# Conditioned decoder trunk on one Trainium2 core: c loaded as columns and broadcast through TensorE, and the first FFN weights in two transfers per k-tile

## The chip, the core and the metric

The kernel runs on one core of one Trainium2 chip. A core has a matrix engine (TensorE, PE in the profile; its weight loads are PEld), a vector engine (VectorE, DVE), a scalar engine (ScalarE, ACT), a general engine (GpSimd, POOL) and a sync engine (SyncE, SP) that here issues nearly all transfers between HBM and on-chip memory. Each engine works through its own list of instructions in order; engines wait for one another, and for transfers, through semaphores. The metric is the device time of one execution in microseconds; 1000.66 us is the median of three executions before the change (999.98 to 1000.76).

## The reference, cut to what matters

Two layers act on x, 256 positions by 1024 channels, all in float32. Each layer is FFN, token mixer, FFN; every sub-layer normalises x, modulates it with a shift and a scale computed from one conditioning vector c, and adds its result through a gate computed from c.

```python
c_act = silu(c)                                  # c: (1, 1024)
mods = c_act @ ada_w[layer] + ada_b[layer]       # nine vectors of 1024 a layer
sh1, sc1, g1, ... = split(mods, 9)
h = rms_norm(x, norm_g) * (1 + sc1) + sh1
x = x + 0.5 * g1 * swiglu(h, w_gate, w_up, w_down)
h = ...                                          # sh2, sc2
x = x + g2 * attention(h)                        # layer 0: MoBA, layer 1: MLA
h = ...                                          # sh3, sc3
x = x + 0.5 * g3 * swiglu(h, ...)
```

The change touches the beginning: silu(c), the shift and the scale of the very first norm, and the first 768 of 2816 columns of the first FFN's gate and up matrices.

## The kernel before

Every float32 product is done with operands split into a rounded high part (`hi`, type float32r) and a remainder (`lo`); ACT makes the high part by a copy and DVE the remainder by a subtraction (`split`, L624 to L629). Weights stream from HBM in 1 MB tiles through three buffers (`rawp`, tag `raw`; `wload`, L727). The matrices for shift, scale and gate stream in 512 KB tiles (`adaw`); a shift or scale column is a DVE product of such a tile with c_b, which holds silu(c) on all 128 partitions, summed along the row (`column`, L635).

The order on each engine isn't the order of the code. `Order` (L244) lists all instructions with their dependences, gives each a modelled cost (`duration`, L199), places them one after the other on the engine that is free first, and fixes the resulting order per engine. `ranked(j)` gives instructions of the beginning a rank that overrides their due time. One item of that model is the cost of a change of ACT's function table, `TABLE` (1280 ns), added whenever the planned function needs the other table (L454 to L456).

The beginning is `first` (L1490). For the first six blocks of 128 FFN columns, gate and up, it works k-tile by k-tile (eight k-tiles of 128 channels), so that work can start as soon as the first k-tile has arrived. In a k-tile stand:

- loads on SP: two `adaw` tiles (shift, scale; 512 KB each, L1523) and the k-tile's weights (`load_w`, L1510), 128 x 1536 elements in three transfers of 256 KB. They lie in pieces of six borrowed buffers, in the places `3 * (k % 6) + j`, so k-tiles 6 and 7 reuse the places of 0 and 1;
- on DVE: two products with c_b (`column`, L1578; the instruction's line is L638), a small one for the scale (L643), then three remainders `wlo` of the weights (L1591) and the remainder of h (L773);
- on ACT: three high parts `whi` (L1590), the modulation `z` of the transposed x (L1581), the high part of h (L772), and for every second k-tile the scaling `y` of x (L1568);
- on PE: 36 products of 256 columns (L1599 to L1601) into six PSUM banks that zero products (L1540) have opened, and the transposes of x (L1564 for the first two k-tiles, by a product with a diagonal matrix `diag` that holds 1/rms; L1569 for the others).

c reaches c_b as follows: a 1 x 1024 row is loaded on ACT's queue (L1515), silu is applied to the row on one partition (L1528), PE multiplies a column of ones with the row, 512 columns at a time (L1532), and ACT copies the two halves from PSUM to c_b (L1533). A second copy of c, in columns (`cact`, 128 x 8, part of the tile `cols`), has its own silu (L1534) and is used by the gates. The norm of x needs a sum of squares for each half t of the positions: t=0 on DVE (L1550), t=1 on ACT (L1547) with a small DVE instruction behind it (L1548); POOL turns them into 1/rms (L794) and ACT into `diag` (L1554).

In the ranks, k-tile k's weights have 2k+3 and its `adaw` tiles 2k+2, but the loads and splits of k-tiles 6 and 7 have rank 2 * KD + 2 = 18, behind the `adaw` tiles of k-tile 7 (rank 16). The 1 MB tiles of the rest of the FFN come after them and need a `raw` buffer that `first` has given back.

## Time and profile before

| | |
|---|---|
| median of three executions | 1000.66 us |
| the profiled execution's own time | 1000.38 us |
| its span, first to last instruction | 998.6 us |
| PE busy | 984.3 us, 99% |
| DVE, ACT, POOL busy | 848.7, 630.1, 82.8 us |
| read from HBM | 255.34 MB, 260 GB/s over the span |

The profile is one execution, taken by the hardware profiler. In the views that follow, a timeline row reads: start in us, length in us, engine (a q behind it means that only the engine's sequencer works: it issues a transfer), line, operation, output tile, input tiles, shape, count of instructions merged, and in brackets how long the engine had been idle and what ended that. A row of the waits reads: who, for whom, us in total, times, longest. A row of the windows gives the busy time of each engine in a stretch of time, then the share of the clock, the busy share of the DMA engines and GB/s.

### The profile page before, as it was taken

The numbers are of one execution on the slowest core, as the hardware profiler recorded it, in microseconds if no ns is written. First come the engines' busy times: TensorE is split into PE (matmuls) and PEld (weight loads), VectorE is DVE, ScalarE is ACT, GpSimd is POOL, SyncE is SP. The second block draws the span as 40 slices with busy tenths as digits, with TensorE's granted clock in tenths as the row PEclk, the third lists the DMA queues.
The fourth block names the chain that finished last, engine by engine and source line by source line (L and its number), as shares of the span: only waits on it lengthen the run. The fifth ranks groups of instructions, "written<-read, shape, count | busy, mean of one in ns | idle before, by whom it ended". The sixth has DMA issues, their size and how long they took to land.

```text
span 998.6 us, 15267 instructions
## 1 busy us (share of the span) xinstructions
PE 984.3 (99%) x5558; PEld 837.0 (84%) x5558; DVE 848.7 (85%) x1442; ACT 630.1 (63%) x1171; POOL 82.8 (8%) x124
## 2 busy tenths in 40 slices
PE   8999999999999999999999999999999999999998
PEld 6988888888888788888888888888888878888886
DVE  7999999799989899999799999944998789677542
ACT  6698564378755876665367665633879686667421
POOL 1012100022230000000000000000143010000000
PEclk9999999999999999999999999999999999999999
DMA  9979989799786679988988989752343467544630
GB/s 366 402 263 298 334 315 347 303 334 350 269 299 238 237 277 331 333 302 317 363 326 315 331 320 326 235 215 98 106 153 127 170 243 273 201 169 170 230 127 21
DMA packets 54237, 260.53 MB, mean 261 GB/s; under 512 B 6289, under 2 KB 6801, under 8 KB 35986
## 3 DMA queue, kind: packets, MB, share of 16 engines
q1 hardware_dynamic: 52704, 255.93, 70.5%
q0 software_dynamic: 1024, 3.17, 1.1%
q8 instruction: 43, 0.70, 0.3%
q10 hardware_dynamic: 434, 0.46, 0.2%
q14 instruction: 32, 0.26, 0.1%
HBM read 255.34 MB, written 4.19 MB: 260 GB/s over the span
## 4 chain that ended last, share of the span: by engine, by line
PE 79%; issue 9%; DVE 6%; DMA 4%; POOL 1%; ACT 1%; SPq 0%; ACTq 0%; DVEq 0%; POOLq 0%
PE mm L957 23%; PE mm L757 12%; PE mm L759 12%; PE mm L758 12%; PE mm L965 12%; DMA adaw<-in_ada_dram 2%; PE at L1013 2%; DVE lo L628 2%; DMA raw<-in_first_dram 1%; PE at L1069 1%; PE at L1049 1%; PE tr L1168 1%; PE tr L807 1%; DMA raw<-in_w_dram 1%; DVE z L823 0%
## 5 line engine op out<-in xcount | busy, mean ns | idle before, releaser
L628 DVE TENSOR_TENSOR lo<-raw,hi 128x1024 fp32r<-128x1024 f32 (+3 forms) x312 | 368.9, 1199 | 71.8 <-ACT hi L627 63.2
L627 ACT ACTIVATE hi<-raw 128x1024 fp32r<-128x1024 f32 (+3 forms) x312 | 318.7, 1038 | 154.2 <-PE mm L759 124.2
L957 PE MATMUL mm<-h,hi 128*128 128x512 f32 x1120 | 288.3, 393 | 0.0
L957 PEld LDWEIGHTS mm<-h,hi 128*128 128x128 f32 x1120 | 199.9, 189 | 34.8
L965 PEld LDWEIGHTS mm<-h,lo 128*128 128x128 f32 x1120 | 155.3, 190 | 12.8 <-DVE lo L628 0.8
L965 PE MATMUL mm<-h,lo 128*128 128x256 f32 x1120 | 162.0, 282 | 0.6 <-DVE lo L628 0.6
L638 DVE CUSTOM_DVE_ANT_0 adaw<-adaw,c_b,cols 128x1024 f32<-128x1024 f32 x112 | 142.0, 1285 | 2.5 <-DMA adaw<-in_ada_dram 1.5
L757 PE MATMUL mm<-hi,gh 128*128 128x512 f32 x352 | 137.3, 390 | 0.0
L759 PE MATMUL mm<-hi,gl 128*128 128x512 f32 x352 | 137.1, 389 | 0.0
L758 PE MATMUL mm<-lo,gh 128*128 128x512 f32 x352 | 137.0, 389 | 0.0
L757 PE MATMUL mm<-hi,h 128*128 128x512 f32 (+1 forms) x240 | 94.7, 400 | 0.8 <-ACT h L772 0.8
L759 PE MATMUL mm<-hi,h 128*128 128x512 f32 (+1 forms) x240 | 92.6, 391 | 1.6 <-DVE h L773 1.6
L758 PE MATMUL mm<-lo,h 128*128 128x512 f32 (+1 forms) x240 | 93.8, 394 | 0.0
L759 PEld LDWEIGHTS mm<-hi,gl 128*128 128x128 f32 x352 | 66.1, 188 | 13.8
L758 PEld LDWEIGHTS mm<-lo,gh 128*128 128x128 f32 x352 | 66.1, 188 | 13.5
L757 PEld LDWEIGHTS mm<-hi,gh 128*128 128x128 f32 x352 | 66.1, 188 | 13.3
L676 DVE SCALAR_TENSOR_TENSOR acc<-adaw,cols,acc 128x1024 f32<-128x1024 f32 x48 | 61.8, 1288 | 0.3
L759 PEld LDWEIGHTS mm<-hi,h 128*128 128x128 f32 x240 | 45.1, 188 | 10.5 <-DVE h L773 2.1
L757 PEld LDWEIGHTS mm<-hi,h 128*128 128x128 f32 x240 | 45.0, 188 | 9.5 <-ACT h L772 1.4
L758 PEld LDWEIGHTS mm<-lo,h 128*128 128x128 f32 x240 | 45.1, 188 | 8.1 <-issue 0.2
L895 ACT ACTIVATE u<-mm 128x256 f32<-128x256 f32 x70 | 26.3, 375 | 32.7 <-PE mm L965 31.7
L772 ACT ACTIVATE gh<-g 128x256 fp32r<-128x256 f32 x76 | 31.4, 413 | 24.4 <-DVE g L899 24.1
(233 smaller groups left out, 1235.1 us busy)
## 6 DMA issues: line engine op xcount, KB each, us to landing
raw<-in_w_dram SPq DMA_DIRECT2D x142, 1024.0 KB, 5.2
adaw<-in_ada_dram SPq DMA_DIRECT2D x160, 512.0 KB, 5.8
raw<-in_first_dram SPq DMA_DIRECT2D x24, 256.0 KB, 7.3
raw<-in_w_dram SPq DMA_DIRECT2D x12, 512.0 KB, 3.5
raw<-in_w_dram SPq DMA_DIRECT2D x6, 576.0 KB, 3.8
bias_d<-bt SPq DMA_DIRECT2D x12, 256.0 KB, 5.5
bg<-bias_d POOLq DMA_DIRECT2D x4, 768.0 KB, 6.4
raw<-in_w_dram SPq DMA_DIRECT2D x2, 768.0 KB, 4.1
```

Source lines behind the costliest of these rows:

```text
L627: nc.scalar.activation(hi, src, AF.Copy)
L628: nc.vector.tensor_tensor(lo, src, hi.bitcast(F32), op=ALU.subtract)
L638: nc.vector.tensor_tensor_reduce(wt, wt, c_b, 1.0, cols[:, i, c:c + 1], op0=ALU.mult, op1=ALU.add, accum_out=m_cols[:, i, c:c + 1])
L676: nc.vector.scalar_tensor_tensor(acc, ada_tile(j, k), cact[:, k:k + 1], acc, op0=ALU.mult, op1=ALU.add)
L757: nc.tensor.matmul(ps, lh, rh, start=start, stop=False)
L758: nc.tensor.matmul(ps, lh, rl, start=False, stop=False)
L759: nc.tensor.matmul(ps, ll, rh, start=False, stop=stop)
L772: nc.scalar.activation(hi, ps, AF.Copy)
L895: nc.scalar.activation(x, ps[:, S:], AF.Copy)
L957: nc.tensor.matmul(ps[i], w[0], hs[2], start=k == 0, stop=False)
L965: nc.tensor.matmul(ps[i][:, S:], w, hk_, start=False, stop=k == KD - 1)
L1013: nc.tensor.matmul(ps3[:, i, :], qTs(e, t), kTs(e, nk), start=bias is not None, stop=bias is not None or i == len(es) - 1)
```

## The change

- c is laid out on the host as 128 rows of 8 values, `cact` becomes a tile of its own, loaded by a transfer of its own on ACT's queue; c is no longer part of `cols`.
- silu is applied once, to `cact`. c_b is made by eight products of 128 columns: the stationary operand is one column of `cact` repeated 128 times, the moving one the identity. The two copies to c_b stay.
- The first weights come in two transfers per k-tile, 1024 and 512 columns (k-tile 0 in three of 512), and their splits have the same pieces. Their places change: k-tiles 6 and 7 no longer lie in the places of 0 and 1 but in those of 3, 4 and 2, and only three, not four k-tiles are loaded without a wait for a norm's instruction.
- Loads and splits of k-tiles 6 and 7 have the ranks of their place: load k+3 is ranked 2k+10 = 2(k+3)+4, split 2k+3.
- In the planner, a table change costs only what ACT's idle time before it doesn't hide.

The planner makes a new order for the whole kernel from this. On PE it has 64 places of difference, on ACT 53, on DVE 139, on SP 25, none on POOL.

```diff
@@ lay_out
-    out["first"] = out["first"].reshape(KD, P, 3, -1).transpose(0, 2, 1, 3)
+    first = out["first"].reshape(KD, P, -1)
+    out["first"] = np.concatenate([first[:, :, :FIRST_A].reshape(KD, -1), first[:, :, FIRST_A:].reshape(KD, -1)], axis=1)
...
-    more = [v["c"].reshape(KD, P).T, pos.view(np.float32).reshape(NT, P).T]
+    out["c"] = v["c"].reshape(KD, P).T
+    more = [pos.view(np.float32).reshape(NT, P).T]
@@ Order.place
             if self.table[k] and self.table[k] != table:
                 table = self.table[k]
-                occ, dur = occ + TABLE, dur + TABLE
+                d = max(0.0, TABLE - (t - idle_from))
+                occ, dur = occ + d, dur + d
...
+            if e == "Activation":
+                idle_from = free[e]
@@ first
-            third = n1 // 3
+            cuts = (0, FIRST_A, n1)
...
-            place = [t[:, c:c + third] for t in raws for c in range(0, t.shape[-1], third)]
+            place = [(r[:, :FIRST_A], r[:, FIRST_A:n1]) for r in raws[:3]]
+            place += [(raws[3 + b], raws[b][:, n1:]) for b in range(3)]
+            place += [(raws[3 + b], raws[2][:, b * 512:(b + 1) * 512]) for b in range(2)]
 
             def load_w(k):
-                for j in range(3):
-                    nc.sync.dma_start(w1(k, j), a["first"][k, j])
+                for w, c, e in zip(place[k], cuts, cuts[1:]):
+                    src = a["first"][k, c * P:e * P].rearrange("(p f) -> p f", p=P)
+                    step = 512 if k == 0 else e - c
+                    for c1 in range(0, e - c, step):
+                        nc.sync.dma_start(w[:, c1:c1 + step], src[:, c1:c1 + step])
 
             with ranked(0):
-                nc.scalar.dma_start(c_b[0:1, :], a["c"])
+                nc.scalar.dma_start(cact, a["c"])
                 nc.scalar.dma_start(all_cols, a["cols"])
...
-                if k < 4:
+                if k < 3:
                     with ranked(2 * k + 3):
                         load_w(k)
             with ranked(0):
-                nc.scalar.activation(c_b[0:1, :], c_b[0:1, :], AF.Silu)
+                nc.scalar.activation(cact, cact, AF.Silu)
                 for i in range(2):
                     pt = tr_tile()
-                    half = slice(i * 512, (i + 1) * 512)
-                    nc.tensor.matmul(pt, ones[0:1, :], c_b[0:1, half], start=True, stop=True)
-                    nc.scalar.activation(c_b[:, half], pt, AF.Copy)
-                nc.scalar.activation(cact, cact, AF.Silu)
+                    for j in range(4):
+                        k = 4 * i + j
+                        nc.tensor.matmul(kslice(pt, j), cact[:, k:k + 1].to_broadcast([P, P]), ident, start=True, stop=True)
+                    nc.scalar.activation(c_b[:, i * 512:(i + 1) * 512], pt, AF.Copy)
...
-            for k in (4, 5):
+            for k in (3, 4, 5):
                 with ranked(2 * k + 3):
                     load_w(k)
...
-                with ranked(2 * k + 3 if k < KD - 2 else 2 * KD + 2):
+                with ranked(2 * k + 3):
                     hi, lo = [fp.tile([P, n1], F32R, tag=g, name=nm(g), bufs=2) for g in ("whi", "wlo")]
-                    for j in range(3):
-                        cs = slice(j * third, (j + 1) * third)
-                        nc.scalar.activation(hi[:, cs], w1(k, j), AF.Copy)
-                        nc.vector.tensor_tensor(lo[:, cs], w1(k, j), hi.bitcast(F32)[:, cs], op=ALU.subtract)
-                if k < 2:
-                    with ranked(2 * KD + 2):
-                        load_w(KD - 2 + k)
+                    for w, c, e in zip(place[k], cuts, cuts[1:]):
+                        step = 512 if k == 0 else e - c
+                        for c1 in range(c, e, step):
+                            cs, src = slice(c1, c1 + step), w[:, c1 - c:c1 - c + step]
+                            nc.scalar.activation(hi[:, cs], src, AF.Copy)
+                            nc.vector.tensor_tensor(lo[:, cs], src, hi.bitcast(F32)[:, cs], op=ALU.subtract)
+                if k in (3, 4):
+                    with ranked(2 * k + 10):
+                        load_w(k + 3)
```

Line numbers below are those of the kernel before; behind the change the same lines stand 7 to 10 further down (L1591 becomes L1601, L638 becomes L645).

What the new order does with the instructions around the change, engine by engine, as the two programs list them:

| engine | before | after |
|---|---|---|
| ACT | load c, load cols, table, silu of the row, silu of cact, square of x (t=1), two copies to c_b, diag, diag, whi x3, z, h | load c, load cols, table, silu of cact, two copies to c_b, square of x (t=1), diag, diag, whi, z, h, whi x2 |
| DVE | ..., the small instruction of t=1 (L1548), column, column, scale, wlo x2, h, wlo | the same small instruction (now L1556), column, column, scale, wlo, h, wlo x2 |
| DVE, first 1 MB tile | lo, 18 other instructions, lo | lo, 2 other instructions, lo |
| SP, end of `first` | adaw of k 6, adaw of k 7, weights of k 6 and 7, 1 MB tile, three adaw tiles, two 1 MB tiles | adaw of k 6, weights of k 6, adaw of k 7, weights of k 7, two 1 MB tiles, three adaw tiles, a 1 MB tile |

More of the change, by code (lines that the diff above doesn't have):

```diff
@@ L31 @@
 B1 = 6
+FIRST_A = 1024
 H = 16
@@ L167, in lay_out @@
     out["tab"] = np.concatenate([*[np.tile(x, (4, 1)) for x in (table[1:], table[:-1], end)], *keys], axis=1)
-    for n in ("x", "c", "positions", "kv_a_norm_g", "mla_q_a_norm_g"):
+    for n in ("x", "positions", "kv_a_norm_g", "mla_q_a_norm_g"):
         out[n] = v[n]
@@ L377, in place @@
             in_pool[r[0]] = in_pool.get(r[0], 0) + users[t]
-        flight, dma_free, dtype, table = [], 0.0, None, None
+        flight, dma_free, dtype, table, idle_from = [], 0.0, None, None, 0.0
         def grant(r):
@@ L610, in trunk @@
     pos_f = a["positions"].rearrange("o s -> (o s)")
-    all_cols = cp.tile([P, 3 * NK + KD + NT + 4 + 2 * RO], F32, name="cols")
+    all_cols = cp.tile([P, 3 * NK + NT + 4 + 2 * RO], F32, name="cols")
+    cact = cp.tile([P, KD], F32, name="cact")
     places = {}
     c0 = 3 * NK
-    for name, n in (("c", KD), ("pos", NT), ("moba_q", 1), ("moba_k", 1), ("q", 1), ("q_pe", RO), ("k", 1), ("k_pe", RO)):
+    for name, n in (("pos", NT), ("moba_q", 1), ("moba_k", 1), ("q", 1), ("q_pe", RO), ("k", 1), ("k_pe", RO)):
         places[name] = all_cols[:, c0:c0 + n]
         c0 += n
-    cols, cact = all_cols[:, :3 * NK].rearrange("p (i c) -> p i c", i=3), places["c"]
+    cols = all_cols[:, :3 * NK].rearrange("p (i c) -> p i c", i=3)
     m_cols = cp.tile([P, 2, NK], F32, name="m_cols")
```

2 lines of the change are left out of this document (removed).

## The prediction

> **What bounds the kernel now.** I read the page first: how much of the span PE is busy.
>
> ```profile
> span 998.6 us, 15267 instructions
> PE 984.3 (99%) x5558; PEld 837.0 (84%) x5558; DVE 848.7 (85%) x1442; ACT 630.1 (63%) x1171; POOL 82.8 (8%) x124
> ```
>
> PE leaves 14.3 us of the span unused, so that's all that an edit which removes no product can win. Where these lie is asked of the windows of the beginning and of PE's own waits, over the whole span and then in 700 to 830, the MLA stage, which gave the same three rows.
>
> ```profile
> core 0: us, PE busy (x) PEld busy (x) DVE busy (x) ACT busy (x) POOL busy (x), PEclk, DMA share, GB/s
> 14.00:18.00 4.00, 4.00 (x36) 4.00 (x35) 4.00 (x10) 2.73 (x5) 0.00 (x0) 1.00 1.04 403
> 38.00:42.00 4.00, 3.50 (x29) 3.29 (x28) 4.00 (x9) 1.87 (x4) 0.00 (x0) 1.00 1.06 392
> 50.00:54.00 4.00, 3.37 (x22) 2.83 (x20) 4.00 (x15) 3.30 (x8) 1.12 (x32) 1.00 0.96 386
> ```
>
> ```profile
> PE mm L759 <- DVE h L773: 1.6, 2, 1.4
> ...
> PE mm L757 <- ACT ckT L772: 0.6, 1, 0.6
> PE mm L757 <- ACT qlT L772: 0.6, 1, 0.6
> ```
>
> In `first`, PE, DVE and the DMA engines are all full at once (4.00 of 4.00 us, share 1.04, 403 GB/s): three limits within a few per cent of one another. PE idles 0.50 us in 38 to 42 and 0.63 us in 50 to 54. The largest waits of PE outside the beginning are in the MLA stage (the L757 and L759 rows, 2.8 us together). The rest of the 14.3 us lies mostly ahead of the first real product. So I read the timeline of the first 13 us, by engine.
>
> ```profile
> 0.74 0.52 ACTq L1515 DMA_DIRECT2D c_b<-in_c_dram  x1
> ...
> 1.69 1.28 ACT L1528 ACT_TABLE_LOAD   x1 [1.69 <-PEq L1641]
> 2.98 1.05 ACT L1528 ACTIVATE c_b<-c_b 1x1024 f32<-1x1024 f32 x1
> 4.09 3.78 PE L1532 MATMUL tr<-c_b,ones_r 1*128 1x512 f32 x4 [1.05 <-ACT c_b L1528]
> 4.39 1.22 DVE L1550 CUSTOM_DVE_ANT_0 raw<-x 128x1024 f32<-128x1024 f32 x1 [2.10 <-DMA x<-in_x_dram]
> 6.09 0.21 ACT L1534 ACTIVATE cols<-cols 128x8 f32<-128x8 f32 x1 [2.06 <-DMA cols<-in_cols_dram]
> 6.21 1.04 ACT L1547 ACTIVATE raw<-x 128x1024 f32<-128x1024 f32 x1
> 7.25 1.25 ACT L1533 ACTIVATE c_b<-tr 128x512 f32<-128x512 f32 x2
> 7.37 0.15 DVE L1548 TENSOR_SCALAR ssq<-ssq 128x1 f32<-128x1 f32 x1 [1.12 <-ACT raw L1547]
> 8.54 1.28 DVE L638 CUSTOM_DVE_ANT_0 adaw<-adaw,c_b,cols 128x1024 f32<-128x1024 f32 x1 [1.01 <-ACT c_b L1533]
> 8.84 2.08 PE L1564 MATMUL tr<-diag,x 128*128 128x128 f32 x8
> 9.24 1.97 ACT L1590 ACTIVATE whi<-raw 128x512 fp32r<-128x512 f32 x3 [0.16 <-DMA raw<-in_first_dram]
> 11.02 1.28 DVE L1591 TENSOR_TENSOR wlo<-raw,whi 128x512 fp32r<-128x512 f32 x2
> 11.21 0.56 ACT L1581 ACTIVATE z<-tr,m_cols 128x256 f32<-128x256 f32 x1
> 11.80 0.42 ACT L772 ACTIVATE h<-z 128x256 fp32r<-128x256 f32 x1
> ...
> 12.27 1.22 PE L1599 MATMUL mm<-h,whi 128*128 128x256 f32 x4 [0.29 <-ACT h L772]
> ```
>
> The chain: silu of the row to 4.03, products to 7.87, copies to 8.50, DVE's columns from 8.54, 2.48 us for two of them and the scale, then z, h and the first product at 12.27. From 8.54 on DVE has hardly a pause until the last remainder.
>
> ```profile
> 13.20 1.28 DVE L638 CUSTOM_DVE_ANT_0 adaw<-adaw,c_b,cols 128x1024 f32<-128x1024 f32 x1
> 15.68 1.29 DVE L1591 TENSOR_TENSOR wlo<-raw,whi 128x512 fp32r<-128x512 f32 x2
> 17.25 0.68 DVE L1591 TENSOR_TENSOR wlo<-raw,whi 128x512 fp32r<-128x512 f32 x1
> 17.86 1.28 DVE L638 CUSTOM_DVE_ANT_0 adaw<-adaw,c_b,cols 128x1024 f32<-128x1024 f32 x1
> 27.25 0.43 DVE L773 TENSOR_TENSOR h<-z,h 128x256 fp32r<-128x256 f32 x1 [0.88 <-ACT h L772]
> 44.96 2.49 DVE L1591 TENSOR_TENSOR wlo<-raw,whi 128x512 fp32r<-128x512 f32 x4
> 47.59 1.22 DVE L628 TENSOR_TENSOR lo<-raw,hi 128x1024 fp32r<-128x1024 f32 x1
> 52.67 1.22 DVE L628 TENSOR_TENSOR lo<-raw,hi 128x1024 fp32r<-128x1024 f32 x1
> ```
>
> A k-tile costs DVE 4.66 us (13.20 to 17.86); its one real pause is 0.88 us at k-tile 3; the last remainder ends at 47.45.
>
> **The change part by part.**
>
> *c to c_b.* When the 128 rows of 8 values land isn't in the trace. From below: silu can't start before the table is loaded, 2.97. From above: x's first half is asked for in the same instant and its consumer starts at 4.39. I take 3.5, a little under the middle, since c is 4 KB and x 512 KB. Silu on 128x8 costs 0.21 (the L1534 row), so PE starts at 3.75. The L1564 row is four products of this size, each two passes: eight passes in 2.08 us. Eight products are twice that less one drain, 3.6 us: nothing is won against 3.78. The first copy now finds ACT free, the second (0.62) ends at 8.05 instead of 8.50: 0.45 early (ends 7.5 and 8.95).
>
> *What is moved behind it.* In the new order ACT does both copies ahead of the square of x (L1547), and on DVE the small L1548 of that square still stands ahead of the first column. So the columns now wait for copies plus square: 8.05 + 1.13 (6.21 to 7.34) + 0.1 = 9.3, against 8.54. **0.75 us later**, although c_b is earlier. The diagonal of t=1 follows at about 10.4 and is hidden by the columns, which end at 11.8.
>
> *k-tile 0.* ACT now does z and h ahead of the second and third whi: z 11.9, h 12.45, whi to 14.05, so DVE's third wlo ends near 14.85 and k-tile 1's columns start at 14.75 instead of 13.20: **1.55 late**, half of it new. PE's first product comes at 12.95 instead of 12.27.
>
> *Two pieces instead of three.* One remainder of 1024 costs 1.22 (the L628 row) against 1.29 for two of 512: 0.07 us for each of seven k-tiles, **-0.5 us**. Two transfers instead of three save SP an issue per k-tile; that is worth nothing, for SP stands waiting for earlier transfers to land:
>
> ```profile
> SPq L1512 <- DMA adaw<-in_ada_dram: 12.9, 13, 2.4
> ```
>
> *The order of the weights.* Whi's waits for these weights, and what SP and PE do at the end of `first`:
>
> ```profile
> ACT whi L1590 <- DMA raw<-in_first_dram: 7.8, 7, 2.1
> ```
>
> ```profile
> 38.72 0.33 SPq L734 DMA_DIRECT2D raw<-in_w_dram  x1
> ...
> 46.32 1.48 SPq L734 DMA_DIRECT2D raw<-in_w_dram  x2
> ```
>
> ```profile
> 50.84 2.00 PE L957 MATMUL mm<-h,hi 128*128 128x512 f32 x8
> 52.68 0.63 PE L965 MATMUL mm<-h,lo 128*128 128x256 f32 x4
> 53.94 0.74 PE L965 MATMUL mm<-h,lo 128*128 128x256 f32 x4 [0.63 <-DVE lo L628]
> ```
>
> The bytes are the same and DMA was full, so nothing lands sooner in total. But DVE comes 1.55 us later to k-tile 1 and 1.3 later to k-tile 3, so its pause there is filled: **-0.9 us**. DVE's last remainder: 47.45 + 1.55 - 0.5 - 0.9 = 47.6, 0.15 later than before. Behind it PE had 3.4 us left (47.45 to 50.84), some 30 products at the 0.11 us that 36 records in 4.00 us give. Now k-tile 6's weights arrive before k-tile 7's columns, and PE has only k-tile 7 at the end: 36 products, of which six or so fit between h and the last remainder (0.7 us). Again 30: no gain. The cover of PE's pause at 41 (0.50) is DVE, which ends last either way.
>
> The gain lies right behind. Two 1 MB tiles go out before DVE is done with k-tile 7, instead of one (38.72) with the next held to 46.32, and DVE's second lo stands two instructions behind the first instead of eighteen. The 0.63 us wait at 53.94 goes: **-0.6 us**. If the second tile were still late, nothing would be won there; if it also helped the next blocks, up to 1.1 us.
>
> *Third load of k-tile 6 and 7 on SP.* They now wait for k-tiles 3 and 4 to be split. By the DVE times above k-tile 3's wide remainder ends near 28, about 1 us before SP would issue at the DMA's pace; nothing, as long as DVE isn't another 1 us late.
>
> *The planner's new price for tables.* The table loads stay five and in their places. The reordered instructions in the MLA stage meet the 2.8 us of waits quoted above: bounds -2.8 and, if the new order lengthens them as much, +2.8. A handful of products moved by a few places either way: I take **-0.3**.
>
> *Sum* against the profiled execution, 1000.38: DVE's end +0.15, behind it -0.6, MLA -0.3, together -0.75: 999.63. The median stands 0.28 above that execution: **999.9 us**.
>
> **The rivals.** (A) c takes turns with x and lands with its first half, 4.4. For it: cols, asked for right behind x's second half, is consumed at 6.09, x's half at 6.21. Columns then start at 10.2; 0.9 of DVE time is added: 1000.8.
>
> The Trainium skill (DMA: Bandwidth & Descriptors, section Queues, rings and completion order) says that each DMA engine takes turns between queue rows, a packet from each. By that rule c would be done with x's first half, 1000.8; the pair 6.09 and 6.21 agrees.
>
> (B) The other side, slower than before: c's short rows are slow in themselves, and c needs what cols needs, from 1.29 to 6.09, 4.8 us: 5.54, which is 2.04 later than assumed, 1001.9. It decides from a landing at 4.3 on (0.76 later gives 1000.66), and past 4.5 SP's load of k-tile 6 waits too. Against it: c is 4 KB, cols 123 KB.
>
> The same page's Specifications put the shortest transfer at full rate at 512 bytes, below which the write becomes a read and a write; that speaks against 32-byte rows, and no row here shows its price.
>
> (C) c lands by 2.97 (0.55 less) and MLA's new order wins half of its waits instead of a tenth (1.1 less): 999.9 - 1.65 = 998.25. For it: c_b's copies were held up by ACT's order, not by c.
>
> (D) The change doesn't do what it says: k-tile 7's data or the second tile's remainder stay last, and the order alone moves: 1000.38 + 0.15 and the median's 0.28, 1000.8.
>
> **How the numbers follow.** Forecast 0.42 (its own range 999.1 to 1000.7), A 0.20, B 0.12, C 0.15, D 0.11. 0.2% is 2.0 us, about what a measurement of this kernel can tell from no change: faster means below 998.66, slower above 1002.66. C's faster part and some tail of the forecast give 0.18; B with its SP wait and an unlucky MLA order 0.10; the rest 0.72. The range, 998.2 to 1001.8, reaches C and B.
>
> **What would show it.** In the profile after: the first column product (L638) at 9.3, behind the small t=1 instruction and that behind the square; the first L1599 product at 12.95; hardly any whi wait for the weights past k-tile 2; the last wlo near 47.5; no 0.63 us wait at the first lo products. Wrong would be: a first column at or before 8.5 (then c_b, not the square, ends last, and C holds); silu of cact after 4.4 (A) or 5 (B); waits of SP's weights of k-tile 6 for a wlo; a PE idle time in 700 to 800 that has changed by more than 1 us.

## The result and the profile after

| | before | after |
|---|---|---|
| median of 13 executions | 1000.20 us (999.25 to 1000.94) | 1002.11 us (1000.34 to 1003.50) |
| ratio, with its 95% interval | | 1.0020 [1.0012, 1.0027] |
| profiled execution, its span | 1000.38, 998.6 | 1003.50, 1001.6 |

The change makes the kernel 1.9 us slower; forecast was 999.9, with 998.2 to 1001.8 as the range. The executions of the changed kernel also lie further apart, 3.2 us instead of 1.7, and the profiled one is the slowest of them, so its 3.0 us of longer span are more than the median's 1.9.

The head of the changed kernel's page, span and busy time of each engine:

```profile
span 1001.6 us, 15255 instructions
PE 983.9 (98%) x5570; PEld 839.8 (84%) x5570; DVE 848.1 (85%) x1435; ACT 627.6 (63%) x1163; POOL 85.1 (8%) x124
```

PE is as busy as before (984.3) and DVE 0.6 us less. The 3 us are pauses. Where they begin stands in the timeline of the first 17 us (start, length, engine, line; in brackets how long the engine had been idle and what ended that):

```profile
4.45 1.23 DVE L1558 CUSTOM_DVE_ANT_0 raw<-x 128x1024 f32<-128x1024 f32 x1 [2.15 <-DMA x<-in_x_dram]
4.66 0.21 ACT L1536 ACTIVATE cact<-cact 128x8 f32<-128x8 f32 x1 [1.72 <-DMA cact<-in_c_dram]
5.01 3.75 PE L1541 MATMUL tr<-ident,cact 128*128 128x128 f32 x16 [2.10 <-ACT cact L1536]
...
8.79 0.60 ACT L1542 ACTIVATE c_b<-tr 128x512 f32<-128x512 f32 x1 [1.10 <-PE tr L1541]
9.29 1.05 ACT L1555 ACTIVATE raw<-x 128x1024 f32<-128x1024 f32 x1
...
10.46 0.15 DVE L1556 TENSOR_SCALAR ssq<-ssq 128x1 f32<-128x1 f32 x1 [3.92 <-ACT raw L1555]
10.53 1.27 DVE L645 CUSTOM_DVE_ANT_0 adaw<-adaw,c_b,cols 128x1024 f32<-128x1024 f32 x1
10.69 1.52 POOL L801 TENSOR_TENSOR rstd<-ssq,mhalf 128x1 f32<-128x1 f32 x1 [4.35 <-DVE ssq L1556]
...
12.25 0.40 ACT L1562 ACTIVATE diag<-ident,rstd 128x128 f32<-128x128 f32 x1 [1.54 <-POOL rstd L801]
...
13.53 0.56 ACT L1589 ACTIVATE z<-tr,m_cols 128x256 f32<-128x256 f32 x1 [0.37 <-PE tr L1572]
...
14.58 0.43 DVE L780 TENSOR_TENSOR h<-z,h 128x256 fp32r<-128x256 f32 x1 [0.69 <-ACT h L779]
...
14.75 0.78 PE L1609 MATMUL mm<-h,whi 128*128 128x256 f32 x2
...
16.31 1.28 DVE L645 CUSTOM_DVE_ANT_0 adaw<-adaw,c_b,cols 128x1024 f32<-128x1024 f32 x1
```

c lands at 4.63, behind x's first half (4.42). DVE stands still for 3.92 us until the square's small instruction, and the first column starts at 10.53 instead of 8.54. POOL's rstd takes 1.52 us. The diagonal made from it then holds z (13.53, released by PE's transposes, not by the columns), and k-tile 1's columns start at 16.31 instead of 13.20.

The windows of both kernels, cut where the lateness is made (0 to 16.5), where it can be made up for (to 50), and where it is paid (to 135). First before, then after; the third pair of numbers behind the bounds is DVE's busy time:

```profile
0.00:16.50 16.50, 14.00 (x57) 8.76 (x58) 10.71 (x24) 11.41 (x21) 3.93 (x26) 1.00 0.92 350
16.50:50.00 33.50, 32.93 (x267) 31.90 (x266) 31.96 (x65) 21.43 (x41) 0.00 (x0) 1.00 1.04 401
50.00:92.00 42.00, 41.37 (x472) 35.31 (x471) 41.38 (x108) 39.53 (x88) 7.34 (x39) 1.00 0.79 276
92.00:135.00 43.00, 42.04 (x238) 36.48 (x237) 41.20 (x59) 27.87 (x50) 7.44 (x8) 1.00 0.91 318
```

```profile
0.00:16.50 16.50, 10.58 (x48) 8.34 (x49) 7.79 (x18) 7.86 (x16) 4.90 (x26) 0.86 0.90 343
16.50:50.00 33.50, 33.50 (x274) 33.50 (x274) 33.40 (x60) 21.53 (x35) 0.00 (x0) 0.96 1.03 405
50.00:92.00 42.00, 42.00 (x478) 36.04 (x477) 40.03 (x109) 38.68 (x88) 7.36 (x37) 1.00 0.74 259
92.00:135.00 43.00, 40.90 (x230) 35.09 (x229) 40.41 (x57) 27.48 (x50) 8.27 (x9) 1.00 0.90 310
```

Take each window's length less DVE's busy time. DVE idles 5.8, 1.5, 0.6 and 1.8 us before, 8.7, 0.1, 2.0 and 2.6 after: 9.7 against 13.4 up to 135 us, 3.6 more. With 0.6 us less DVE work that is the 3.0 us of the span. This says where the time lies, not yet which engine sets the end. Note the last two rows of after: PE is full from 50 to 92 and loses 2.1 us from 92 to 135. That loss stands in the waits of PE, with those of the MLA stage below it, which are the ones of before to the tenth:

```profile
PE mm L964 <- DVE g L903: 1.6, 2, 1.1
PE mm L766 <- DVE h L780: 1.6, 2, 1.4
...
PE mm L764 <- ACT ckT L779: 0.6, 1, 0.6
PE mm L764 <- ACT qlT L779: 0.6, 1, 0.6
...
PE mm L964 <- DVE u L903: 0.5, 1, 0.5
```

One of DVE's late pauses has a cause of its own. On SP's queue the last store of the bias table goes out right behind a 1 MB weight tile, and ACT, then DVE, wait for it (timeline of after; the store issued at 99.13 landed at 107.97):

```profile
98.70 0.33 SPq L741 DMA_DIRECT2D raw<-in_w_dram  x1
...
99.13 0.83 SPq L1183 DMA_DIRECT2D bias_d<-bt  x1
...
108.15 0.42 ACT L779 ACTIVATE gh<-g 128x256 fp32r<-128x256 f32 x1 [3.14 <-DMA bias_d<-bt]
108.47 1.04 ACT L634 ACTIVATE hi<-raw 128x1024 fp32r<-128x1024 f32 x1
108.59 0.43 DVE L780 TENSOR_TENSOR gl<-g,gh 128x256 fp32r<-128x256 f32 x1 [1.68 <-ACT gh L779]
```

### The profile page after: what moved, and what is told of

Read it like the earlier page. It is cut to its first block, busy times and chain, and to the rows that moved or that the text cites. A ratio compares the mean times of both kernels' runs of the same rounds, so it can differ in the third digit from the quotient of the medians.

```text
span 1001.6 us, 15255 instructions
## 1 busy us (share of the span) xinstructions
PE 983.9 (98%) x5570; PEld 839.8 (84%) x5570; DVE 848.1 (85%) x1435; ACT 627.6 (63%) x1163; POOL 85.1 (8%) x124
## 3 DMA queue, kind: packets, MB, share of 16 engines
q0 software_dynamic: 1024, 3.17, 1.0%
## 4 chain that ended last, share of the span: by engine, by line
PE 83%; issue 9%; DVE 5%; POOL 1%; ACT 1%; DMA 0%; DVEq 0%; ACTq 0%; POOLq 0%
PE mm L964 24%; PE mm L764 12%; PE mm L972 12%; PE mm L765 12%; PE mm L766 12%; PE at L1020 2%; PE at L1076 1%; DVE lo L635 1%; PE tr L1175 1%; PE at L1056 1%; PE mm L1609 1%; PE tr L814 1%; PE mm L1610 1%; PE mm L1611 1%; DVE z L830 0%
## 5 line engine op out<-in xcount | busy, mean ns | idle before, releaser
L645 DVE CUSTOM_DVE_ANT_0 adaw<-adaw,c_b,cols 128x1024 f32<-128x1024 f32 x112 | 141.9, 1283 | 0.5 <-DMA adaw<-in_ada_dram 0.5
L765 PEld LDWEIGHTS mm<-lo,gh 128*128 128x128 f32 x352 | 66.1, 188 | 13.4
L683 DVE SCALAR_TENSOR_TENSOR acc<-adaw,cact,acc 128x1024 f32<-128x1024 f32 x48 | 61.4, 1280 | 1.0 <-DMA adaw<-in_ada_dram 0.7
L766 PEld LDWEIGHTS mm<-hi,h 128*128 128x128 f32 x240 | 45.1, 188 | 10.4 <-DVE h L780 2.2
L801 POOL TENSOR_TENSOR rstd<-ssq,mhalf 128x1 f32<-128x1 f32 x12 | 12.2, 1016 | 418.6 <-DVE ssq L796 386.7
```

Source lines behind the costliest of these rows:

```text
L645: nc.vector.tensor_tensor_reduce(wt, wt, c_b, 1.0, cols[:, i, c:c + 1], op0=ALU.mult, op1=ALU.add, accum_out=m_cols[:, i, c:c + 1])
L683: nc.vector.scalar_tensor_tensor(acc, ada_tile(j, k), cact[:, k:k + 1], acc, op0=ALU.mult, op1=ALU.add)
L765: nc.tensor.matmul(ps, lh, rl, start=False, stop=False)
L766: nc.tensor.matmul(ps, ll, rh, start=False, stop=stop)
L801: nc.gpsimd.tensor_tensor(r, stats[t], mhalf[:, 0:1], op=ALU.pow)
```

## The experiments

The theories, by the names that the expectations use: **late beginning** (what counts is how late DVE comes to its columns), **order of the later loads** (the new order of SP behind `first` costs), **clock** (PE's slower products), **takes turns** and **short rows** (why c lands late), and later **two late places** (the beginning, and the bias table's store). The table gives every run's profiled DVE idle time, worked out from its windows as above, and its span less that idle time. A ratio is to the kernel before in the same series, whose median was 1000.28 beside e1 to e4, 1000.13 beside e5 to e8, 1000.16 beside e9 to e12 and 999.97 beside e13 to e15.

| kernel | median (range) | ratio to before, 95% | DVE idle 0-16.5, -50, -92, -135 | sum | span | span less idle |
|---|---|---|---|---|---|---|
| before | 1000.20 (999.25-1000.94) | | 5.8, 1.5, 0.6, 1.8 | 9.7 | 998.6 | 988.9 |
| after | 1002.11 (1000.34-1003.50) | 1.0020 [1.0012, 1.0027] | 8.7, 0.1, 2.0, 2.6 | 13.4 | 1001.6 | 988.2 |
| e1 c as a row | 999.98 (998.62-1000.67) | 0.9998 [0.9989, 1.0007] | 6.2, 1.1, 0.4, 1.5 | 9.2 | 998.0 | 988.8 |
| e2 price of a table | 1000.49 (998.89-1003.64) | 1.0005 [0.9997, 1.0014] | 6.5, 0.4, 1.7, 2.3 | 10.9 | 999.4 | 988.5 |
| e3 square on DVE | 1000.35 (998.92-1002.58) | 1.0004 [0.9995, 1.0012] | 6.5, 0.1, 1.6, 1.2 | 9.4 | 999.1 | 989.7 |
| e4 weights alone | 1000.31 (998.91-1001.81) | 1.0005 [0.9996, 1.0013] | 6.3, 1.2, 0.8, 1.5 | 9.8 | 998.5 | 988.7 |
| e5 c first | 1000.28 (998.80-1001.70) | 1.0001 [0.9993, 1.0010] | 7.1, 0.5, 1.1, 0.3 | 8.9 | 997.2 | 988.3 |
| e6 c first, square on DVE | 1000.57 (998.58-1002.37) | 1.0006 [0.9997, 1.0015] | 5.3, 0.9, 1.6, 3.0 | 10.8 | 1000.6 | 989.8 |
| e7 extra DVE work at 74 us | 1001.57 (1000.46-1002.57) | 1.0013 [1.0004, 1.0022] | 5.8, 1.6, 0.6, 0.1 | 8.1 | 999.3 | 991.2 |
| e8 the same at 435 us | 1000.45 (999.10-1000.90) | 1.0003 [0.9995, 1.0012] | 5.8, 1.5, 0.6, 0.7 | 8.6 | 997.3 | 988.7 |
| e9 after, stores by POOL | 1003.04 (1002.24-1003.50) | 1.0028 [1.0017, 1.0039] | 8.5, 0.1, 1.6, 2.2 | 12.4 | 1000.9 | 988.5 |
| e10 before, stores by POOL | 1001.03 (1000.74-1002.04) | 1.0010 [1.0001, 1.0019] | 5.8, 1.7, 1.7, 1.9 | 11.1 | 1000.0 | 988.9 |
| e11 c first, stores by POOL | 1001.60 (1000.75-1003.86) | 1.0019 [1.0010, 1.0027] | 7.2, 0.7, 1.6, 1.0 | 10.5 | 998.8 | 988.3 |
| e12 the same, square on DVE | 1001.74 (1000.65-1002.94) | 1.0016 [1.0008, 1.0025] | 5.5, 0.7, 1.8, 1.0 | 9.0 | 999.4 | 990.4 |
| e13 after, no last store | 1001.23 (999.66-1001.98) | 1.0009 [1.0000, 1.0019] | 8.7, 0.1, 1.6, 1.3 | 11.7 | 1000.1 | 988.4 |
| e14 c first, no last store | 1000.20 (999.18-1001.90) | 1.0003 [0.9994, 1.0012] | 7.4, 0.7, 0.9, 1.5 | 10.5 | 999.3 | 988.8 |
| e15 before, no last store | 999.99 (999.17-1000.68) | 1.0000 [0.9992, 1.0009] | 5.8, 1.6, 0.6, 1.3 | 9.3 | 998.2 | 988.9 |

The last column is 988.2 to 988.9 wherever DVE has its usual work up to 135 us. It is 989.7 to 990.4 in the three kernels that give DVE a square of 1.2 us more (e3, e6, e12), and 991.2 where it has 2.4 us more (e7). So the profiled spans differ by what DVE does and by how long it stands still up to 135 us; behind that all kernels take nearly the same time. This column alone can't say that DVE is the cause. PE and DVE wait for one another there, and an engine that keeps step with the end gives such a column whatever it waits for. The same difference with PE's idle time runs from 992.2 to 994.3, less even, but of the same kind.

Two things say that **up to 130 us it is mostly DVE that PE waits for**, although PE looks full: in the profiles every wait of PE between 50 and 135 us ends with a DVE instruction, and e7 below makes DVE's work longer and the kernel slower. It isn't so in every execution: in those profiled of e5 and e8 PE has no pause at all from 92 to 135 us. And it holds for a late beginning: one better than that of the kernel before gains nothing (e6). The idle times are those of one execution and change from one to the next; medians are compared by themselves.

**e1: the part on c undone.** In the changed kernel:

```diff
-                nc.scalar.dma_start(cact, a["c"])
+                nc.scalar.dma_start(c_b[0:1, :], a["c"])
...
-                        nc.tensor.matmul(kslice(pt, j), cact[:, k:k + 1].to_broadcast([P, P]), ident, start=True, stop=True)
+                    nc.tensor.matmul(pt, ones[0:1, :], c_b[0:1, half], start=True, stop=True)
```

> The changed kernel with the part on c undone (row, silu of the row, product of ones with the row, cact inside cols); new weights' order and new price of a table stay. Theory 'late beginning' (the 2.1 us by which the changed kernel misses my forecast stand in its first 16 us: the first column comes at 10.53 instead of 8.54, k-tile 1's columns at 16.31 instead of 13.20): the first column returns to about 8.6, k-tile 1's columns to about 13.3, the last wlo ends by 47.5, and the median is 999.5 to 1000.3, 2 us under the changed kernel. Theory 'order of the later loads' (the three adaw tiles and the positions behind the two 1 MB tiles cost PE its time between 80 and 140 us): the beginning is early again, but the median stays at 1001.5 to 1002.5. Theory 'clock' (PE's slower products up to 18 us and the spread of 1000.3 to 1003.5 come from pauses of PE in the beginning): as 'late beginning', and the spread of the runs shrinks to under 2 us.

Measured 999.98, the first column at 8.84, k-tile 1's columns at 13.69, the last wlo's end at 47.24. SP's order is that of the changed kernel to about 90 us, with the positions and the three adaw tiles behind the two 1 MB tiles; from there on the new plan differs, and the last store of the bias table no longer has a 1 MB tile right ahead of it. e2 keeps SP's order to 257 us, and e3 and e5 (but for c's own load) to the end, and they come down as well. So that order by itself doesn't cost 2 us: the late beginning does.

**e2: the price of a table undone.**

```diff
-                d = max(0.0, TABLE - (t - idle_from))
-                occ, dur = occ + d, dur + d
+                occ, dur = occ + TABLE, dur + TABLE
```

> The changed kernel with the full price of a table in the plan again; columns of c and weights' order stay. The plan then puts the square of x (t=1) between the two copies. 'Late beginning': c still lands near 4.6 and c_b is complete near 9.4, but the square is done by 8.9, so rstd runs ahead of DVE's first column and takes 0.55 us as before; first column near 9.5, first L1609 product near 13.9, k-tile 1's columns near 14.5 (half of the 3.1 us lost), median 1000.8 to 1001.3. 'Order of the later loads': SP's order is that of the changed kernel, so 1001.8 to 1002.5. If the price of a table were itself the cause (MLA stage), 1000.2.

Measured 1000.49, a little under the expected 1000.8. The planner now puts the square between the two copies. c lands as late as in the changed kernel, but rstd starts before the first column (timeline of e2):

```profile
9.00 0.55 POOL L798 TENSOR_TENSOR rstd<-ssq,mhalf 128x1 f32<-128x1 f32 x1 [2.61 <-DVE ssq L1553]
9.17 0.82 ACT L1559 ACTIVATE diag<-ident,rstd 128x128 f32<-128x128 f32 x2
9.31 1.28 DVE L642 CUSTOM_DVE_ANT_0 adaw<-adaw,c_b,cols 128x1024 f32<-128x1024 f32 x1 [0.39 <-ACT c_b L1539]
```

So the price of a table, which I had looked for in the MLA stage, does its work in the first 10 us: it decides whether ACT copies or squares first.

**e3: the square of t=1 on DVE.**

```diff
-                    if t:
-                        nc.scalar.activation(junk, xs[t], AF.Square, scale=D ** -0.5, accum_out=s)
...
+                    nc.vector.tensor_tensor_reduce(junk, xs[t], xs[t], 1.0 / D, EPS, op0=ALU.mult, op1=ALU.add,
+                                                   accum_out=s)
```

> The changed kernel with the square of x (t=1) on DVE, which is idle there from 5.7 to 10.4, instead of ACT. 'Late beginning', its part from the order on ACT: the square ends near 7.4, rstd of t=1 runs alone (0.55 us), the first column waits for the second copy alone (9.4), k-tile 1's columns near 14.5, PE's first L1609 product near 13.0; median 1000.7 to 1001.3. If instead c's landing (4.63) is all that counts, the first column stays past 10.2 and the time at 1002. 'Order of the later loads': 1002.

Measured 1000.35. The square's 1.2 us fill DVE's idle time and rstd runs alone (timeline of e3):

```profile
7.90 0.55 POOL L801 TENSOR_TENSOR rstd<-ssq,mhalf 128x1 f32<-128x1 f32 x1 [1.30 <-DVE ssq L1554]
...
9.64 1.29 DVE L645 CUSTOM_DVE_ANT_0 adaw<-adaw,c_b,cols 128x1024 f32<-128x1024 f32 x1 [1.83 <-ACT c_b L1542]
```

k-tile 1's columns start at 15.09, 0.6 later than expected, and still 1.8 us of the median come back.

**e4: the weights' order and pieces alone** (e1 and e2 together).

> The changed weights' order and pieces alone: c as a row and the price of a table as before. 'Late beginning': the beginning is that of before (first column 8.5, k-tile 1's columns 13.2), DVE's pause at k-tile 3 is smaller or gone, last wlo at or under 47.5, the wait of 0.63 us at the first lo products gone: 999.4 to 1000.2, not slower than before. 'Order of the later loads': this edit is the cause, 1001.5 to 1002.5.

Measured 1000.31, just above the expected range: neither the gain of 0.6 that the forecast gave to this order nor a clear loss. The last wlo ends at 46.90, 0.55 earlier than before, and DVE's idle time is the same, 9.8 against 9.7: 0.3 us less from 16.5 to 50 and again from 92 to 135, 0.7 more in the other two windows, most of it before 16.5. What is won at the last wlo doesn't reach the end: the span is 998.5 against 998.6. PE's pauses move instead, from 0.63 to 0 us between 50 and 92 and from 0.96 to 2.02 between 92 and 135.

**e5: c loaded by SP ahead of x.**

```diff
-                nc.scalar.dma_start(cact, a["c"])
+                nc.sync.dma_start(cact, a["c"])
```

> The changed kernel with c's load on SP's queue ahead of x instead of on ACT's; cact stays 128 rows of 8. It asks why c landed at 4.63, 0.2 behind x's first half (4.42). 'Takes turns' (rival A of the prediction: its 128 short rows share the DMA engines with x's first half): ahead of x it lands by 3.3, silu starts by 3.3, the products near 3.6, c_b is complete near 8.0. 'Short rows' (rival B: 32-byte rows are slow in themselves): it still lands at 4.4 or later and c_b is complete at 9.2 or later. If the first column then starts by 8.2, 'late beginning' asks for k-tile 1's columns by 14.0 and a median of 999.4 to 1000.4, at least 1.5 us under the changed kernel.

Timeline of e5:

```profile
2.79 0.21 ACT L1536 ACTIVATE cact<-cact 128x8 f32<-128x8 f32 x1 [0.33 <-DMA cact<-in_c_dram]
...
6.94 0.60 ACT L1542 ACTIVATE c_b<-tr 128x512 f32<-128x512 f32 x1 [1.11 <-PE tr L1541]
...
8.35 1.28 DVE L645 CUSTOM_DVE_ANT_0 adaw<-adaw,c_b,cols 128x1024 f32<-128x1024 f32 x1 [2.24 <-DMA adaw<-in_ada_dram]
...
9.79 1.53 POOL L801 TENSOR_TENSOR rstd<-ssq,mhalf 128x1 f32<-128x1 f32 x1 [3.02 <-DVE ssq L1556]
```

The same 128 short rows land at 2.77 instead of 4.63: they aren't slow in themselves, and beside x they were held up. The median comes down to 1000.28. Now the first column waits for its own tile (adaw), and rstd starts inside a column again and takes 1.53 us, so k-tile 1's columns come at 14.81, not by 14.0. It isn't faster than the kernel before.

**e6: both.** The diffs of e5 and e3.

> The same, and the square of x (t=1) on DVE, so that both copies stand first on ACT and nothing of the norm stands ahead of them. 'Takes turns': c_b complete near 8.0, the first column at 8.0 (the first adaw tile lands at 7.6), earlier than in any kernel so far; k-tile 1's columns at 13.0. DVE's idle time up to 135 us, 9.5 in the kernel before and 13.1 in the changed one, would be under 9. If DVE is what ends last up to 130 us, the median is 998.8 to 999.8; if PE's or the DMA's own work is (full from 16 to 50 us), 1000.0 to 1000.5 whatever the beginning does.

Measured 1000.57: a miss for DVE as what sets the end (998.8 to 999.8), and next to the 1000.0 to 1000.5 of the other theory, by which PE or the DMA does. The beginning is the best of all, 5.3 us idle, and nothing comes of it. Part of the lead is lost because ACT's high parts wait for weights (1.4 us at 10.2, 1.5 at 15.4). In the profiled execution, the slowest of its runs, the rest is given back behind 50 us: ACT's gh waits 4.0 us for the last store of the bias table, and DVE behind it 1.7.

**e7 and e8: 2.4 us more DVE work in the kernel before, at 74 and at 435 us.**

```diff
-        nc.vector.tensor_tensor(lo, src, hi.bitcast(F32), op=ALU.subtract)
+        n_split[0] += 1
+        for i in range(3 if n_split[0] == 12 else 1):
+            nc.vector.tensor_tensor(lo, src, hi.bitcast(F32), op=ALU.subtract)
```

(200 in place of 12 in e8.)

> The kernel before with one remainder of 1024 columns on DVE near 74 us computed three times instead of once: 2.4 us more of DVE work, nothing else. My forecast treated DVE work behind the first stage as hidden (PE busy 30.00 of 30.00 us from 50 to 80). 'DVE ends last up to 130 us' (all kernels so far differ in their end as they differ in DVE's idle time up to 135 us): the time grows by 1.4 to 2.4 us, to 1001.7 to 1002.7, less only by what DVE's 1.0 us pause at 98.7 takes up. 'PE ends last there': 1000.0 to 1000.6.

> The control: the same 2.4 us of extra DVE work, but at the 200th split, near 435 us, where DVE is busy 92 of 100 us and PE 100 of 100. Here both theories say that PE ends last: 1000.0 to 1000.6, no more than 0.3 above the kernel before. If it costs 1 us or more too, extra DVE work costs everywhere and the place near 74 us shows nothing.

Near 74 us the extra work costs 1.44 us (1001.57 against 1000.13 of the same series), the lower end of what was expected if DVE sets the end there (1.4 to 2.4). The rest went into pauses: from 92 to 135 DVE is busy for 42.90 of 43 us (window of e7), 41.20 before.

```profile
92.00:135.00 43.00, 42.38 (x239) 36.78 (x239) 42.90 (x64) 27.79 (x49) 7.63 (x8) 1.00 0.92 326
```

Near 435 us it costs 0.32, inside its interval. There DVE is busy 92 of 100 us and its extra work doesn't reach the end; in the window above it mostly did, at 41.20 of 43. The busy share alone doesn't tell. The traces agree: the remainder lo<-acc near 120 us, up to which e8 is the kernel before, ends at 120.0 in e8, 121.4 in the kernel before and 122.6 in e7, and the spans are 997.3, 998.6 and 999.3.

**e9 to e12: the bias table's stores issued by POOL**, in the changed kernel, the kernel before, e5 and e6.

```diff
-                nc.sync.dma_start(bias_d[t + kb, c], bt.rearrange("p h k -> p (h k)"))
+                nc.gpsimd.dma_start(bias_d[t + kb, c], bt.rearrange("p h k -> p (h k)"))
```

> The changed kernel with the stores of the bias table (bias_d<-bt) issued by POOL instead of SP, nothing else. In the changed kernel's profile ACT stands still for 3.1 us until 108.1 (gh, released by the last of these stores: issued on SP's queue at 99.13 right behind a 1 MB tile, landed at 107.97), DVE then 1.7 us behind ACT. Theory 'two late places': DVE's busy time ends last up to 135 us, and of the 3.6 us that DVE idles more than in the kernel before (13.4 against 9.7), 2.9 us come from the beginning and the rest from later waits, among them this store. The wait of gh for bias_d goes, DVE's idle time from 92 to 135 falls from 2.6 to 1.0 or less, the median to 1000.3 to 1001.2, and the runs spread less than the 3.2 us of the changed kernel. 'Late beginning alone': the store's wait is hidden or its place is taken by another wait, 1001.7 to 1002.3.

> The kernel before with the same edit, as the control. In its profile no engine waits for these stores. 'Two late places': no gain from it, 999.8 to 1000.4. If it gains as much as in the changed kernel, the store is not what the changed kernel pays for.

> Both late places mended in the changed kernel: c loaded by SP ahead of x, and the bias table's stores issued by POOL. 'Two late places': the median falls to the fast end of the kernel with c first alone, 998.6 to 999.6, the runs above 1001 vanish, and it is faster than the kernel before. If the beginning and the store are not what spreads the runs, 1000.0 to 1000.5 as with c first alone.

> The same and the square of x (t=1) on DVE: first column at 8.3, rstd of t=1 outside a column (0.55 instead of 1.53 us), DVE idle up to 16.5 us 5.3 instead of 7.1. 'Two late places': 998.3 to 999.4, the best so far, DVE idle up to 135 us at 8 or under. If DMA or PE ends last from 16 to 50 us, no better than c first with the stores on POOL.

All four are slower than expected, the control too, 0.9 us slower than the kernel before. The edit neither took ACT's wait away (still 3.6 us in e9) nor was free: with POOL as the issuer a buffer of the table comes back later, ACT waits for a store near 74 us and DVE behind it (timeline of e10). These four say nothing on the question they were made for.

```profile
74.06 0.60 ACT L1172 ACTIVATE bt<-tr 128x512 f32<-128x512 f32 x1 [1.13 <-DMA bias_d<-bt]
...
74.97 0.42 DVE L896 TENSOR_TENSOR u<-mm,u 128x256 f32<-128x256 f32 x1 [1.01 <-ACT u L895]
```

**e13 to e15: without the last store**, in the changed kernel, e5 and the kernel before. The last quarter of the table's last block isn't stored, the third is stored twice, so the kernel computes with other values there.

```diff
-                nc.sync.dma_start(bias_d[t + kb, c], bt.rearrange("p h k -> p (h k)"))
+                for c1 in (c,) if kb == 0 or c < 2 else (2, 3) if c == 2 else ():
+                    nc.sync.dma_start(bias_d[t + kb, c1], bt.rearrange("p h k -> p (h k)"))
```

> The changed kernel without its last store of the bias table: the last quarter of the last block (t=1) isn't stored, the third quarter is stored twice instead, in its place and 3 us earlier, on SP as before; so one quarter of one block of the bias table holds other values. Moving the stores to POOL had left ACT's wait in place (3.6 us) and so had not answered this. 'Two late places': gh on ACT no longer waits for the store landing at 107.97, DVE's idle time from 92 to 135 falls from 2.6 to about 1.3, and the median from 1002.1 to 1000.9 to 1001.5; the runs spread under 2.5 us. 'Late beginning alone': the wait's place is taken by another one, 1001.8 to 1002.4, with the same spread of 3 us.

> The same with c loaded by SP ahead of x (one quarter of one block of the bias table holds other values). With c first alone the runs went from 998.8 to 1001.7 around 1000.28. 'Two late places': the slow part of these runs goes, 999.0 to 999.8. 'Late beginning alone': 1000.0 to 1000.5.

> The control: the kernel before with the same edit (one quarter of one block of the bias table holds other values). Its ACT never waits for a store of the table. 'Two late places' and 'late beginning alone': 999.9 to 1000.4. A gain of 0.5 or more would say that the edit itself saves time, wherever it is made.

In the changed kernel the median falls by 0.9 us to 1001.23 and the runs span 2.3 instead of 3.2 us. Its window from 92 to 135:

```profile
92.00:135.00 43.00, 41.89 (x239) 36.35 (x238) 41.66 (x60) 28.59 (x51) 8.27 (x9) 1.00 0.89 317
```

ACT's wait for the store is gone, and DVE idles 1.3 us there instead of 2.6. But the intervals of the two ratios overlap ([1.0000, 1.0019] and [1.0012, 1.0027]), so a gain isn't shown beyond doubt. The control doesn't move (999.99), and with c first there is next to nothing to win (1000.20 against 1000.28; 999.0 to 999.8 was expected, a miss). So the store is one place at which a late beginning may be paid, and how much of the 1.9 us it makes stays open. It doesn't hang on the late beginning alone: ACT waits for this store in the profiles of e2, e3 and e6 too (2.8, 1.9 and 4.0 us), whose medians are level with the kernel before, and not in that of e5.

None of these kernels is faster than the kernel before. e1, the changed kernel without its part on c, is level with it (0.9998 [0.9989, 1.0007]).

## Why the prediction was wrong

**c to c_b: the term that was mis-sized first.** I took 3.5 for c's landing, between 2.97 and 4.39; it is 4.63, 0.2 above the upper bound. That moves the first column from the forecast 9.3 to 10.53. The mechanism of rival A is the right one (e5: 2.77 when asked for ahead of x). Its own sign, silu of cact after 4.4, came: 4.66. The reason I gave against it, 4 KB beside 512 KB, was none: here the number of rows counted. In the trace of after the transfer's 128 packets of 32 bytes take 9 ns each but are spread from 2.64 to 4.01 us, among x's packets of 4096 bytes and 159 ns; in e5 they pass from 1.73 to 2.38. Most of the rows in after stand in strings of up to eight, some 168 ns apart, the 159 of one of x's packets and the 9 of a row: one of each in turn. That explains the spread; that the first row goes 0.9 us later than in e5, behind 32 of x's packets, isn't explained. A single row of 4 KB, asked for in the same instant, isn't held up in this way (e4: silu at 3.18).

The Trainium skill (DMA: Bandwidth & Descriptors, section Queues, rings and completion order) has it that a DMA engine takes turns between queues; the spread of the packets agrees. The same section of the Trainium skill has the engine empty a whole packet, some 9 to 17 descriptors, before it switches. The trace of after shows one row and one of x's packets in turn instead, and the measurement decides.

**"The diagonal of t=1 follows at about 10.4 and is hidden by the columns": failed.** It follows at 12.25 and holds z to 13.53, while the columns were done at 13.0. I had taken rstd's 0.55 us from a place where DVE stood still. The trace of before shows both prices, alone and started inside one of DVE's wide two-source instructions:

```profile
7.61 0.55 POOL L794 TENSOR_TENSOR rstd<-ssq,mhalf 128x1 f32<-128x1 f32 x1 [1.33 <-DVE ssq L1548]
```

```profile
208.06 1.22 DVE L628 TENSOR_TENSOR lo<-acc,hi 128x1024 fp32r<-128x1024 f32 x1
208.22 1.48 POOL L794 TENSOR_TENSOR rstd<-ssq,mhalf 128x1 f32<-128x1 f32 x1 [81.14 <-DVE ssq L789]
```

The Trainium skill (SBUF — State Buffer, section SBUF: two separate sides) states that DVE and GpSimd share one pair of ports as a lock, and that who starts second is blocked until the other has ended, for a DVE instruction with two inputs among others. The traces agree for POOL: 1.48 and 1.52 us when rstd starts inside such an instruction, 0.55 when it starts 0.31 us ahead of it (e2). That DVE in its turn is blocked isn't seen: the column that starts inside those 0.55 us takes its usual 1.28.

**"Moved behind it" and k-tile 0** were right as mechanisms: the order of ACT and DVE is the one described, and e2 and e3, which change that order, bring 1.6 and 1.8 of the 1.9 us back. (The planner moves other instructions with it: in e3 the order differs from the changed kernel's in some two dozen places each on ACT and on DVE, and nowhere on SP.) Counted from the first column, k-tile 1's columns come 5.8 us later, 5.45 were forecast; the rest of the difference, 1.2 us, is c.

**Two pieces, and the pause at k-tile 3**: right. DVE has 0.6 us less work (0.5 forecast), and its pauses from 16.5 to 50 fall from 1.5 to 0.1, by 1.4 where 0.9 was forecast. The last wlo still ends at 48.92, 1.47 later than before instead of 0.15: most of the 1.56 us by which k-tile 1's columns came later than forecast (16.31 against 14.75) is still there.

**"The gain lies right behind", -0.6: the sum was wrong in kind.** The 0.63 us wait is gone from the profile, as forecast. But I summed PE's waits without asking what PE meets next: in e4, which has this order alone, PE wins 0.63 us at 54 and loses 1.06 more between 92 and 135, and the interval of its time leaves no room for a gain of 0.6. The kernel before had a wait for DVE there (its timeline), with DVE busy 41.38 of 42 and 41.20 of 43 us around it. I passed over it, though its 1.0 us is longer than the 0.63 that I counted and than any wait in the MLA stage but one.

```profile
121.42 0.50 PE L687 MATMUL adaps<-lo,ones_r 128*128 128x512 f32 x1 [0.96 <-DVE lo L628]
```

e7 shows that DVE's time counts there. The +0.15 for DVE's end was passed on to the end of the kernel in full, and that was right in kind: with +1.47 in its place and nothing for the -0.6 and the -0.3, the forecast's own sum gives 1002.1, the measured median. That it fits to a tenth is luck, for the 1.47 comes from one execution, the slowest of 13.

**SP's k-tile 6** had "about 1 us" of margin. K-tile 3's wide remainder ended at 29.44, 1.4 us behind the forecast's 28, and SP waited 0.3 us for DVE, without harm that can be seen: ACT waits for no weight of `first` behind k-tile 1.

**The price of tables, -0.3 in the MLA stage**: nothing there. The edit acts in the first 10 us (e2): it sets the order of copies and square, which the prediction read off the plan without asking which edit made it.

**The 14.3 us that PE leaves unused** were misread too, without a term of the sum hanging on it: 2.5 us of them lie ahead of the first real product (12.27), not most of what the named waits leave. 4.0 lie in 700 to 830, and 4.8 behind 830, where PE's last product ends that long before the span does.

**The rivals.** A is right about c, and its 1000.8 is too low because it stands on the forecast's sum. Without that sum's -0.6 and -0.3 it is 1001.7, with 0.23 for a landing at 4.63 instead of 4.4 it is 1001.9, and with the 0.33 of the diagonal 1002.3; measured were 1002.1. B gives 1001.9, the nearest number, by luck: e5 rules its mechanism out. C needed an early c, and D the 0.63 us wait, which is gone.

What stays open: why a beginning earlier than that of the kernel before gains nothing (e6), the last store's share, and why the kernels with c as columns spread more (2.3 to 4.8 us, but for e9) than those with the row (1.3 to 2.9). The last store may account for part of it in the changed kernel (2.3 us without it). PE's granted clock is lower in 0 to 16.5 us (0.86 against 1.00), but that isn't what decides. e9's profiled execution has the clock at 1.00 there and the same beginning (z 3.01 us behind the first column, 3.00 in after) and is no faster, and e5's has the mean clock of after's (0.997) and the shortest span of all.

## What to carry to other kernels

Find the engine that sets the end of a stage by adding work to it, not by the busy share: in the kernel before PE was busy for 98% of 50 to 135 us, and yet 2.4 us more of DVE's work cost 1.4. A gain of PE in front of a place where it waits for another engine can be given back there, as in e4. Take the price of an operation from a row in which its neighbours are the ones it will have, since the same instruction cost 0.55 and 1.5 us depending on what DVE was doing when it started. And before a small transfer is split into many short rows, look at what is asked for in the same instant: here its rows went one by one between the large ones.

## What the runs showed of the hardware that was not expected

- Short rows: 32-byte packets took 9 ns each, so the rows cost little; asked for beside x instead of ahead of it, they landed 1.9 us later (4.63 against 2.77), one row and one 159 ns packet of x in turn.
- POOL's operation on 128x1 ended 0.4 us after the DVE instruction it had started in, though the next column (11.73 to 13.01) was already running, and that column took its usual 1.28 us.
- cols, 122 KB in 952-byte rows, landed at 2.92 when it was asked for first, 0.44 us ahead of x (e6), and at 6.36 when it was second on its queue and behind x (after). Which of the two made the difference isn't shown.
